# A two-layer hybrid encoder on one core: another beginning, and fused attention logits with VectorE doing the minimum and the division

## The chip, the cores and the metric

One Trainium2 chip, of which one core is used. The kernel is one program, written out without loops for that core. The metric is the device time of one execution, in microseconds. The engines are named as in the profile: PE is TensorE (matrix products), PEld its weight loads, DVE is VectorE, ACT is ScalarE, POOL is GpSimd, SP is SyncE. A small q behind a name (SPq) is the engine's sequencer, which issues DMAs and waits.

## The reference

Two layers of the same block run over two groups of tokens that share the weights: a prompt of 512 tokens and a sample of 32 tokens that continues a cache of 256. The model width is 1024, everything is float32. One layer is, with P = rmsnorm(x) @ w_in split by columns:

```
A: u = glu_a * sigmoid(glu_b); causal depthwise convolution (31 taps); layernorm; swish; @ w_conv_out
B: rotary(q), rotary(k), retention in chunks with decay (8 heads of 64); groupnorm; * silu(gate); @ w_ret_out
C: rmsnorm per head of q and k; forgetting attention, 8 heads of 64:
     s = q.k/8 + cum(logf)_query - cum(logf)_key, masked causally; softmax(s) @ v; @ w_fox_out
x = x + (sig(gA)*A + sig(gB)*B + sig(gC)*C) @ w_out
x = x + (gelu(causal dwconv3(h W_a)) * (h W_b)) @ W_down,  h = rmsnorm(x)
```

The outputs are both groups' x and the new states (convolution tails, retention states, keys, values, log forget gates).

## The kernel before, in words

Activations lie transposed: 128 channels on the partitions, the 544 tokens (32 + 512) along the free side, so 1024 channels are eight tiles of 128 x 544. Every float32 product is made of three fast ones: a matrix is split into a high part (rounded to the fast format) and a low part (what is left), and `gemm` (line 310 issues its products) adds high x high, high x low and low x high into one PSUM tile `acc`, in two halves of 272 columns. A product of the trace is thus 128 x 128 weights by 272 columns; a weight "unit" of eight 128 x 128 blocks is 48 of them. There are 2 of these PSUM tiles, so the unit after next waits until a result has been copied out.

The weights come as a stream of units (`Stream`, lines 182 to 240). `load` brings a unit from memory into `raw` (SyncE's queue, 2 buffers); `split_part` makes `hi` by a copy on ScalarE (line 203). For the low part there are two ways: usually ScalarE writes `lo = -hi` (line 206) and a DMA issued by GpSimd adds the weights from memory to it (line 207); with `sub` given, VectorE subtracts (line 209). `ahead` splits one unit and loads three units in front of the one in use.

The beginning (lines 405 to 428) loads the input tiles `xk`, the layer's parameters `par` and the first units, splits each input tile with its gain (`norm.split`, ScalarE line 328 and VectorE line 329), and squares the tiles for the norm: two on ScalarE (line 379), six on GpSimd (line 377), added up by VectorE (line 381). `norm.finish` multiplies the sum of squares with a matrix of ones (line 391) and takes the root; the result `R` scales what the products yield, so products can start before it is known. The first two units' results are therefore copied out of PSUM unscaled by ScalarE (line 449). Unit 2 and those behind it take the usual way with the GpSimd DMA.

After a unit's products `slot` hands the result to a function that evicts it. Side work (the depthwise convolution, line 488, the attention, the retention) is written as generators that `tick` advances a step at a time between pieces of the products, and `after(fn, n)` runs a function n units later. The program's text gives the priority; a planner that simulates the engines may move an instruction ahead on its engine's queue where its operands are ready early.

The attention (`fox_side`) works through 32 tiles of the prompt in each layer, one per head and query block of 128; the tile of query block qb has n = 128 (qb + 1) keys, so 128, 256, 384 or 512 columns. `p_scores` makes the products of queries and keys (line 747); VectorE writes the negated logit, key bias minus query bias minus product (line 753), adds a mask of 1e30 on the last 128 columns (line 754) and takes the minimum along the row (line 680). ScalarE makes exp(minimum - logit) with its sum (line 682), VectorE takes 1/sum (line 684), ScalarE multiplies by it (line 685). `p_trans` transposes the tile on TensorE (line 761; one PSUM tile, emptied by ScalarE at line 763), `p_pv` multiplies with the values (line 779). Three steps lie between a tile's logits and its transposes. The key biases are rows read back from memory and spread over the partitions (`ck`). Beside it run the convolution of 31 taps (VectorE line 488, partly ScalarE 491 and GpSimd 495) and the rotary turns, whose halves are swapped by DMAs (line 808) and multiplied and added on GpSimd (lines 811 and 813).

## Time and profile before

| | |
|---|---|
| median of 3 runs | 1995.84 us (1991.99 to 1999.47) |
| the profiled execution | 1999.15 us, its span 1997.0 us |
| mean granted TensorE clock | 0.991 of full speed |
| busy: PE / PEld | 1951.2 / 1909.6 us |
| busy: ACT / DVE / POOL | 1062.5 / 950.5 / 425.3 us |

How to read it: the span is the time from the first to the last instruction of one profiled execution. Busy times are shares of it, but matrix products are pipelined and their ends are modelled, so TensorE's pace is better read from how many products fall into a stretch. A row of a group of instructions gives the line, the engine, the operation, output<-input, the shapes, the count, then the busy time in us and the mean duration of one in ns, and behind the last bar the time in us that the engine was idle before them and what ended it. The chain of waits goes back from the last instruction, at each step to what released it; "issue" in it is time in which the engine waited for nothing that the profile shows.

### The profile page before, as it was taken

To read this page: it belongs to the slowest core of one execution; us is meant where nothing else is said; L and a number is where in the kernel's file an instruction comes from. 1 tells how busy PE (TensorE), PEld (TensorE's weight loads), DVE (VectorE), ACT (ScalarE), POOL (GpSimd) and SP (SyncE) were. 2 spreads that over 40 slices of the span, in tenths; PEclk is the share of its full clock that TensorE was granted. 3 is DMA by queue.
4 is the path that set the end of the run, shared out by engine and by line. 5 is a ranking of instruction groups with operands and counts; after the bars stand their busy time and mean duration, and the time that the engine had idled before them with its cause. 6 is when DMAs were issued, how large, how long until landed. Compare 5 with 4: busy or idle time off the path is not lost.

```text
span 1997.0 us, 37750 instructions
## 1 busy us (share of the span) xinstructions
PE 1951.2 (98%) x15832; PEld 1909.6 (96%) x15832; DVE 950.5 (48%) x1641; ACT 1062.5 (53%) x1462; POOL 425.3 (21%) x580
## 2 busy tenths in 40 slices
PE   7999999999999999999999998999999999999999
PEld 6999889999999999999999987999999999999999
DVE  4377978555234330233224869784543343303330
ACT  5475664476455543454555666636654554434442
POOL 2142422121111221122112334121211122112211
PEclk8999999999999999999999999999999999999999
DMA  7786646567787787787987775556778877777786
GB/s 226 173 186 163 155 106 135 133 153 164 177 218 175 173 179 174 174 176 176 209 205 160 191 172 127 127 122 146 152 169 197 197 175 174 178 173 177 174 184 141
DMA packets 105717, 337.91 MB, mean 169 GB/s; under 512 B 17628, under 2 KB 19276, under 8 KB 105164
## 3 DMA queue, kind: packets, MB, share of 16 engines
q0 software_dynamic: 41760, 152.06, 45.6%
q1 hardware_dynamic: 63788, 183.44, 27.8%
q8 instruction: 124, 2.03, 0.4%
q14 instruction: 45, 0.37, 0.1%
HBM read 321.11 MB, written 9.89 MB: 166 GB/s over the span
## 4 chain that ended last, share of the span: by engine, by line
PE 80%; issue 6%; DVE 6%; ACT 2%; DMA 2%; POOL 2%; SPq 1%; DVEq 0%; POOLq 0%; ACTq 0%
PE acc L310 75%; DVE w L488 3%; DMA lo<-in_wpack_dram 1%; PE s L747 1%; DMA w<-q 1%; PE o L779 1%; DVE w L754 1%; PE t L761 1%; DVE w L753 1%; POOL lo L207 1%; DMA w<-cscr 0%; DVE mn L680 0%; POOL w L377 0%; ACT lo L206 0%; PE s L866 0%
## 5 line engine op out<-in xcount | busy, mean ns | idle before, releaser
L310 PE MATMUL acc<-q,hi 128*128 128x272 f32 x9344 | 1791.3, 291 | 12.7 <-ACT q L328 7.6
L310 PEld LDWEIGHTS acc<-q,hi 128*128 128x128 f32 x9344 | 1478.4, 190 | 27.1 <-ACT q L328 8.7
L310 PE MATMUL acc<-q,lo 128*128 128x272 f32 x4672 | 1352.2, 290 | 5.7 <-DMA lo<-in_wpack_dram 5.4
L310 PEld LDWEIGHTS acc<-q,lo 128*128 128x128 f32 x4672 | 884.4, 190 | 6.8 <-DMA lo<-in_wpack_dram 6.3
L203 ACT ACTIVATE hi<-raw 128x1024 fp32r<-128x1024 f32 (+1 forms) x293 | 309.8, 1057 | 655.5 <-PE acc L310 654.0
L207 POOL DMA_DIRECT2D lo<-in_wpack_dram x290 | 251.7, 868 | 1264.6 <-ACT lo L206 1174.9
L206 ACT ACTIVATE lo<-hi 128x1024 fp32r<-128x1024 f32 x290 | 305.1, 1052 | 4.4
L488 DVE SCALAR_TENSOR_TENSOR w<-w,par 128x574 f32<-128x574 f32 x208 | 198.4, 954 | 3.8
L1177 DVE TENSOR_TENSOR q<-acc,q 128x544 f32<-128x544 f32 x32 | 23.2, 725 | 218.6 <-PE acc L310 218.6
L399 DVE TENSOR_TENSOR w<-acc,R 128x544 f32<-128x544 f32 x94 | 67.7, 720 | 120.2 <-PE acc L310 118.4
L1136 DVE TENSOR_TENSOR w<-acc,R 128x32 f32<-128x32 f32 x44 | 8.5, 192 | 154.6 <-PE acc L310 154.1
L1144 DVE SCALAR_TENSOR_TENSOR w<-w,par 128x546 f32<-128x546 f32 x44 | 34.7, 788 | 83.5 <-ACT w L1143 83.5
L1146 ACT ACTIVATE w<-w 128x546 f32<-128x546 f32 x44 | 29.1, 662 | 70.5 <-DVE w L1145 70.5
L682 ACT ACTIVATE w<-w,mn 128x128 f32<-128x128 f32 (+4 forms) x68 | 37.7, 555 | 31.4 <-DVE mn L680 29.0
L326 DVE TENSOR_TENSOR q<-w,q 128x544 fp32r<-128x544 f32 x44 | 31.9, 725 | 33.7 <-ACT q L325 33.7
L335 DVE TENSOR_TENSOR wr<-w,wr 128x544 fp32r<-128x544 f32 x24 | 26.5, 1104 | 42.7 <-ACT wr L334 42.7
L495 POOL TENSOR_TENSOR w<-w 128x574 f32<-128x574 f32 x24 | 40.1, 1670 | 19.8 <-ACT w L491 19.2
L357 DVE SCALAR_TENSOR_TENSOR w<-s,w 128x272 f32<-128x272 f32 (+1 forms) x60 | 23.6, 435 | 43.4 <-ACT w L354 42.9
L1016 DVE SCALAR_TENSOR_TENSOR w<-w,acc 128x544 f32<-128x544 f32 x32 | 23.0, 720 | 43.6 <-PE acc L310 43.3
L685 ACT ACTIVATE w<-w,rs 128x128 f32<-128x128 f32 (+4 forms) x68 | 37.4, 554 | 9.6 <-DVE rs L684 9.2
L753 DVE SCALAR_TENSOR_TENSOR w<-ck,CM,s 128x128 f32<-128x128 f32 (+3 forms) x64 | 34.3, 536 | 13.4 <-PE s L747 13.4
L811 POOL TENSOR_TENSOR w<-w,cst 128x544 f32<-128x544 f32 x16 | 27.1, 1693 | 56.4 <-DMA w<-q 56.4
(203 smaller groups left out, 1434.7 us busy)
## 6 DMA issues: line engine op xcount, KB each, us to landing
raw<-in_wpack_dram SPq DMA_DIRECT2D x291, 512.0 KB, 3.4
lo<-in_wpack_dram POOLq DMA_DIRECT2D x290, 512.0 KB, 5.5
w<-in_x_dram SPq DMA_DIRECT2D x16, 272.0 KB, 5.2
out_dram<-w SPq DMA_DIRECT2D x16, 272.0 KB, 4.7
w<-q SPq DMA_DIRECT2D x64, 68.0 KB, 4.0
ck<-cscr SPq DMA_DIRECT2D x16, 256.0 KB, 4.2
xn<-q SPq DMA_DIRECT2D x8, 272.0 KB, 5.3
w<-xn SPq DMA_DIRECT2D x8, 272.0 KB, 5.8
```

Of the source, the lines that this page charges most:

```text
L203: act(hi[:, sl], self.raw[u][:, sl], AF.Copy)
L206: act(lo[:, sl], hi[:, sl].bitcast(F32), AF.Copy, scale=-1.0)
L207: nc.gpsimd.dma_start(lo[:, sl], wpack[u][:, sl], accum_op=ALU.add)
L310: mm(acc[:, h, :HN], w, half(x, h), start=(i == 0 and j == 0), stop=(i == n - 1 and j == len(passes) - 1))
L326: vtt(lo, src, hi.bitcast(F32), op=ALU.subtract)
L399: vtt(two(out), acc, two(self.R), op=ALU.mult)
L488: stt(c, u[:, k : k + CO], pcol(w + k), c, op0=ALU.mult, op1=ALU.add)
L495: gtt(p, p, t, op=ALU.add)
L682: act(L[:, :n], L[:, :n], AF.Exp, scale=-1.0, bias=mn, accum_out=sm)
L685: act(L[:, :n], L[:, :n], AF.Copy, scale=rs)
L753: stt(L[:, :n], c[:, :n], CM[:, h, qb : qb + 1], p[:, :n], op0=ALU.subtract, op1=ALU.subtract)
L1144: stt(c, a[:, 1 : 1 + FO], pcol(w + 1), c, op0=ALU.mult, op1=ALU.add)
```

## The change

In the beginning, 14 products of ones with ones are issued into a PSUM tile that nobody reads. The order of loads, splits and squares is fixed as it is written (`manual_schedule`). The parameters and unit 0's weights are loaded by ScalarE's queue; the inputs and units 1 to 3 by SyncE's, unit 2 into a tile of another pool. Units 1 and 2 are split with VectorE's subtraction. All eight squares are ScalarE's. The constants, one load before, become three, pinned in SyncE's queue behind units 4 to 6. In the attention, the factor of the queries is negated and the query's bias left out (a constant along a row falls out of the softmax). VectorE's `tensor_tensor_reduce` adds product and key bias and takes the minimum at once: over the first n - 128 columns with the bias, over the last 128 with bias plus mask, which GpSimd adds beforehand (`ck_diag`). The multiply by 1/sum is VectorE's. The values' transposes in the attention use the PSUM bank `o` in place of `s`; the tag `vs` has one buffer in place of two. A zero fill on GpSimd, the load of the cache and a product with the retention state are pinned to their place in the program.

```diff
-            dma(self.raw[u][:, sl], wpack[u][:, sl])
+            (eng or dma)(self.raw[u][:, sl], wpack[u][:, sl])
...
-    act(warm, epst, AF.Copy)
-    dma(xk[0], x_in[:, 0, :])
-    ws.load_part(0, 0)
-    dma(par, params[0])
...
-    after(lambda: (tc.keep_in_program_order(dma(cst, consts)), act(blkr, blk, AF.Copy)), 3)
...
-    ws.split_part(1, 0, vtt, 1)
-    for k in range(8):
-        norm.square(k, xk[k], k not in (0, 1))
+    adma = nc.scalar.dma_start
+
+    junk = psT_t()
+    for _ in range(14):
+        mm(junk[:, 0:P], ones, ones, start=True, stop=True)
+    with tc.manual_schedule():
+        adma(par, params[0])
+        for k in range(3):
+            dma(xk[k], x_in[:, k, :])
+        ws.load_part(0, 0, eng=adma)
+        ws.load_part(0, 1, eng=adma)
+        act(warm, epst, AF.Copy)
+        for k in range(3, 8):
+            dma(xk[k], x_in[:, k, :])
+        ws.load(3)
+        norm.split(0, xk[0])
+        ws.split_part(0, 0, vtt)
+        norm.split(1, xk[1])
+        norm.split(2, xk[2])
+        ws.split_part(0, 1, vtt)
+        for k in range(3, 8):
+            norm.split(k, xk[k])
+        for u in (1, 2):
+            ws.split_part(u, 0, vtt, 1)
+        for k in range(8):
+            norm.square(k, xk[k])
+
+    def load_consts(a, b):
+        after(lambda: tc.keep_in_program_order(dma(cst[:, a:b], consts[:, a:b])), 4)
+
+    after(lambda: load_consts(C_DQ, C_ALL), 1)
+    after(lambda: load_consts(C_M2, C_DQ), 2)
+    after(lambda: load_consts(0, C_M2), 3)
...
-        nc.gpsimd.memset(fwr.bitcast(F32), 0.0)
+        tc.keep_in_program_order(nc.gpsimd.memset(fwr.bitcast(F32), 0.0))
...
-                    t = psS_t()
+                    t = bank()
...
-        nc.vector.tensor_scalar(gq8, pcol(P_GQ), 0.125, None, op0=ALU.mult)
+        nc.vector.tensor_scalar(gq8, pcol(P_GQ), -0.125, None, op0=ALU.mult)
...
+            def ck_diag(h, qb):
+
+                if h < 8 and (h, qb) not in ckm:
+                    t = wpool.tile([P, P], F32, tag="cm", name="cm", bufs=4)
+                    gtt(t, ck(h)[:, qb * P : (qb + 1) * P], cmask, op=ALU.add)
+                    ckm[h, qb] = t
+                return ckm.get((h, qb))
...
-                act(L[:, :n], L[:, :n], AF.Copy, scale=rs)
+                nc.vector.tensor_scalar(L[:, :n], L[:, :n], rs, None, op0=ALU.mult)
...
-                stt(L[:, :n], c[:, :n], CM[:, h, qb : qb + 1], p[:, :n], op0=ALU.subtract, op1=ALU.subtract)
-                vtt(L[:, n - P : n], L[:, n - P : n], cmask, op=ALU.add)
-                softmax(L, n)
+
+                m = ck_diag(h, qb)
+                if qb < 3:
+                    ck_diag(h, qb + 1)
+                mn = [spool.tile([P, 1], F32, tag="mn" + x, name="mn", bufs=4) for x in "ab"]
+                at = BIG
+                for x, o, e, t in ((c[:, : n - P], 0, n - P, mn[0]), (m, n - P, n, mn[1])):
+                    if e > o:
+                        nc.vector.tensor_tensor_reduce(L[:, o:e], x, p[:, o:e], 1.0, at, ALU.add, ALU.min, t)
+                        at = t
+                softmax(L, n, mn[1])
+                if qb == 1 and h % 2 and h < 7:
+                    ck(h + 1)
+                if qb == 3 and h % 2 == 0 and h < 6:
+                    ck(h + 3)
+                if qb == 3 and h % 2 and h < 7:
+                    ck_diag(h + 1, 0)
+                    ck_diag(h + 2, 0)
```

## Rows read from the trace of the kernel before

**Rows 1.** The page, part 1: busy us, share of the span and instructions of each engine.

```profile
PE 1951.2 (98%) x15832; PEld 1909.6 (96%) x15832; DVE 950.5 (48%) x1641; ACT 1062.5 (53%) x1462; POOL 425.3 (21%) x580
```

**Rows 2.** The chain of waits in order of time: start us, us, what. One run of weight products in the feed-forward part.

```profile
617.22 396.86 PE acc L310 x3168
```

**Rows 3.** Busy time of each engine by stretches (instructions in brackets), then the granted TensorE clock, the DMA share and GB/s.

```profile
130.00:170.00 40.00, 36.49 (x288) 35.62 (x287) 37.14 (x43) 22.20 (x34) 14.12 (x15) 0.96 0.83 211
170.00:265.00 95.00, 88.15 (x725) 78.11 (x724) 75.47 (x158) 59.72 (x133) 38.09 (x28) 0.96 0.59 138
...
490.00:1020.00 530.00, 530.00 (x4227) 529.69 (x4226) 169.75 (x295) 261.59 (x301) 94.96 (x177) 1.00 0.82 186
```

**Rows 4.** Groups of instructions from 0 to 45 us: the weight products, by which half of the weights they use.

```profile
L310 PE MATMUL acc<-q,hi 128*128 128x272 f32 x110 | 26.1, 350 | 9.5 <-ACT q L328 6.2 <-DVE q L329 3.4
...
L310 PE MATMUL acc<-q,lo 128*128 128x272 f32 x54 | 16.1, 343 | 5.4 <-DMA lo<-in_wpack_dram 5.4
```

**Rows 5.** The chain of waits in order of time, cut at 45 us.

```profile
24.20 8.90 DMA lo<-in_wpack_dram
33.14 2.63 PE acc L310 x10
35.78 1.81 PE s L391 x4
37.59 7.49 PE acc L310 x55
```

**Rows 6.** TensorE's instructions in order of time, up to 45 us: start us, us, what, and in square brackets the idle time before and what ended it.

```profile
12.54 0.39 PE L310 MATMUL acc<-q,hi 128*128 128x272 f32 x1 [1.09 <-DVE q L329]
...
15.60 0.59 PE L310 MATMUL acc<-q,hi 128*128 128x272 f32 x1 [2.05 <-DVE q L329]
...
20.98 4.52 PE L310 MATMUL acc<-q,hi 128*128 128x272 f32 x32
...
33.14 0.59 PE L310 MATMUL acc<-q,lo 128*128 128x272 f32 x1 [5.39 <-DMA lo<-in_wpack_dram]
```

**Rows 7.** Stretches of 10 us, columns as in rows 3.

```profile
10.00:20.00 10.00, 6.86 (x32) 6.32 (x31) 9.90 (x10) 3.67 (x6) 7.20 (x6) 0.75 0.67 238
...
30.00:40.00 10.00, 6.86 (x30) 6.39 (x31) 0.90 (x3) 3.81 (x6) 1.16 (x2) 0.66 1.03 333
```

**Rows 8.** The parameters' load in SyncE's queue, and ScalarE's first split that waits for it (in order of time, from two answers).

```profile
1.65 0.43 SPq L411 DMA_DIRECT2D par<-in_params_dram  x1
...
5.38 0.75 ACT L328 ACTIVATE q<-w,par 128x544 fp32r<-128x544 f32 x1 [0.36 <-DMA par<-in_params_dram]
```

**Rows 9.** Groups of instructions: the first four from 0 to 45 us (VectorE's and ScalarE's half of an input split, a half unit's and a unit's high part), the others from the whole trace.

```profile
L329 DVE SCALAR_TENSOR_TENSOR q<-w,par,q 128x544 fp32r<-128x544 f32 x8 | 9.2, 1177 | 0.2 <-ACT q L328 0.2
L328 ACT ACTIVATE q<-w,par 128x544 fp32r<-128x544 f32 x8 | 5.6, 741 | 0.8 <-DMA par<-in_params_dram 0.4 <-DMA w<-in_x_dram 0.2
L203 ACT ACTIVATE hi<-raw 128x512 fp32r<-128x512 f32 x2 | 1.3, 630 | 0.2
L203 ACT ACTIVATE hi<-raw 128x1024 fp32r<-128x1024 f32 x5 | 5.3, 1057 | 4.2 <-PE acc L310 3.4 <-DMA raw<-in_wpack_dram 0.8
...
L329 DVE SCALAR_TENSOR_TENSOR q<-q,par 128x544 fp32r<-128x544 f32 x24 | 18.8, 785 | 21.9 <-ACT q L328 21.9
...
L379 ACT ACTIVATE w<-q 128x544 f32<-128x544 f32 x21 | 13.5, 643 | 0.0
```

**Rows 10.** The GpSimd DMAs of line 207 over the whole trace, 290 of them.

```profile
DMA to landing us min/median/max: 5.0/5.5/9.1
```

**Rows 11.** The attention's operations over the whole trace. First three lines of code with least, median and longest duration in ns; then groups (mean ns behind the busy time); the last is a multiply by scalars in the convolution.

```profile
L753 DVE SCALAR_TENSOR_TENSOR w<-ck,CM,s x64: 319/534/750, 175.3 to 1268.8; 128x128 f32<-128x128 f32 x16, 128x256 f32<-128x256 f32 x16, 128x384 f32<-128x384 f32 x16, 128x512 f32<-128x512 f32 x16
L754 DVE TENSOR_TENSOR w<-w,cst x64: 266/284/1495, 175.7 to 1270.0; 128x128 f32<-128x128 f32 x64
L680 DVE TENSOR_REDUCE mn<-w x68: 257/453/687, 171.7 to 1270.9; 128x1 f32<-128x128 f32 x16, 128x1 f32<-128x256 f32 x16, 128x1 f32<-128x384 f32 x16, 128x1 f32<-128x512 f32 x16
...
L754 DVE TENSOR_TENSOR w<-w,cst 128x128 f32<-128x128 f32 x64 | 29.2, 456 | 0.8
L753 DVE SCALAR_TENSOR_TENSOR w<-ck,CM,s 128x256 f32<-128x256 f32 x16 | 7.5, 472 | 4.1 <-PE s L747 4.1
L753 DVE SCALAR_TENSOR_TENSOR w<-ck,CM,s 128x128 f32<-128x128 f32 x16 | 5.4, 337 | 2.2 <-PE s L747 2.2
L685 ACT ACTIVATE w<-w,rs 128x128 f32<-128x128 f32 (+4 forms) x68 | 37.4, 554 | 9.6 <-DVE rs L684 9.2
L486 DVE TENSOR_SCALAR w<-w,par 128x574 f32<-128x574 f32 x8 | 4.6, 570 | 0.0
```

**Rows 12.** The chain of waits by line, share of the stretch: first 130 to 300 us, then 1110 to 1270 us.

```profile
by line: PE acc L310 30.2%; DVE w L488 10.7%; issue 10.0%; DMA w<-q 5.7%; DVE w L754 4.5%; DVE w L753 3.6%; PE o L779 3.5%; DVE mn L680 3.5%; PE t L761 3.4%; PE s L747 3.0%; DMA w<-cscr 3.0%; SPq L808 2.2%; DVE q L812 2.0%; SPq L662 1.5%; A
...
by line: PE acc L310 32.8%; issue 10.5%; DVE w L488 10.1%; PE s L747 5.4%; PE t L761 3.5%; DVE w L754 3.3%; PE o L779 3.1%; DMA w<-cscr 2.7%; DVE w L753 2.6%; DMA w<-q 2.3%; DVE mn L680 2.2%; SPq L662 2.1%; DVE q L812 1.7%; SPq L808 1.5%; P
```

**Rows 13.** Groups: GpSimd's rotary multiplies over the whole trace, and VectorE's 1/sum from 170 to 265 us, one per tile.

```profile
L811 POOL TENSOR_TENSOR w<-w,cst 128x544 f32<-128x544 f32 x16 | 27.1, 1693 | 56.4 <-DMA w<-q 56.4
...
L684 DVE RECIPROCAL rs<-sm 128x1 f32<-128x1 f32 x26 | 4.1, 158 | 6.8 <-ACT w L682 6.7
```

**Rows 14.** What TensorE waited for over the whole trace: us in total, times, longest us.

```profile
PE t L761 <- ACT w L763: 5.1, 4, 1.9
PE s L625 <- DVE w L357: 4.2, 2, 2.1
```

More of the change, by code (lines that the diff above doesn't have):

```diff
@@ L407, in trunk @@
     warm = cpool.tile([P, 1], F32, name="warm")
-    act(warm, epst, AF.Copy)
-    dma(xk[0], x_in[:, 0, :])
-    ws.load_part(0, 0)
-    dma(par, params[0])
-    for k in (1, 2):
-        dma(xk[k], x_in[:, k, :])
-    ws.load_part(0, 1)
-    for k in range(3, 8):
-        dma(xk[k], x_in[:, k, :])
-    ws.load(1)
-    after(lambda: (tc.keep_in_program_order(dma(cst, consts)), act(blkr, blk, AF.Copy)), 3)
-    norm.split(0, xk[0])
-    ws.split_part(0, 0, vtt)
-    norm.split(1, xk[1])
-    norm.split(2, xk[2])
-    ws.split_part(0, 1, vtt)
-    for k in range(3, 8):
-        norm.split(k, xk[k])
-    ws.split_part(1, 0, vtt, 1)
-    for k in range(8):
-        norm.square(k, xk[k], k not in (0, 1))
+    adma = nc.scalar.dma_start
[28 more added lines that the diff above has]
+    after(lambda: load_consts(0, C_M2), 3)
+    after(lambda: act(blkr, blk, AF.Copy), 6)
     for l in range(DEPTH):
@@ L613, in qk_done, with v_done @@
             return done
-        def v_done(vt, vs, j, out):
+        def v_done(vt, vs, j, out, bank):
             def done(acc):
@@ L648, in trunk @@
         extra_n[0] = 1
-        fvs = spool.tile([P, 512], F32, tag="vs", name="vs")
+        fvs = spool.tile([P, 512], F32, tag="vs", name="vs", bufs=1)
         for j in range(4):
-            slot(rhs, v_done(fv, fvs, j, o_fv[l]))
+            slot(rhs, v_done(fv, fvs, j, o_fv[l], psO_t))
         foh, fol = qhl
```

25 lines of the change are left out of this document (15 added, 10 removed).

## The prediction

> **What bounds the kernel now.** I read the page's totals first, then the engines' busy time by stretches, then the chain of work that ended last. TensorE is busy for 98% of the span [rows 1], but its ends are modelled, so I count products instead. In the long feed-forward run 3168 weight products follow each other in 396.86 us, 0.1253 us each [rows 2]; from 490 to 1020 us no engine but TensorE matters, at full clock [rows 3]. Time can be gained where that pace is missed: in the beginning, and from 130 to about 300 us (and once more in the second layer), where VectorE is 93% and 79% busy [rows 3].
>
> The beginning: up to 45 us the trace has 110 + 54 = 164 weight products [rows 4], worth 164 x 0.1253 = 20.5 us, and four passes over a matrix of ones, 1.81 us at half clock [rows 5], so about 0.9. The chain ends that part at 37.59 + 7.49 = 45.08 us [rows 5]. So 45.1 - 21.4 = 23.7 us are lost there, in three ways. First, the input splits: TensorE idles 6.2 us at first [rows 4] and 2.05 us before 15.60 [rows 6]. Second, the clock: from 10 to 20 us it was granted 0.75 of full speed, from 30 to 40 us 0.66 [rows 7], that is, at the lower of its two levels (1.2 and 2.4 GHz) for part of the time; the ten products from 33.14 took 2.63 us [rows 5] and not 1.25. It fell after the idle 2.05 us and after 5.39 us, and after 15.60 it was back for the run that begins at 20.98, while after the idle 1.09 us before 12.54 the products were quick [rows 6]. Third, the low half of the third weight unit, which a GpSimd DMA adds up: issued at 24.20, landed 8.90 us later [rows 5], and TensorE waited 5.39 us for it [rows 6].
>
> **The change, part by part.** *The beginning.* (a) Parameters and the first weights go to ScalarE's queue, so parameters are issued first and not third. Before, they were issued at 1.65 and awaited until 5.38 [rows 8]; 3.7 us from a first issue at about 0.75 gives 4.5, 0.9 us earlier. The first activation split follows it. (b) The squares leave GpSimd. With GpSimd adding beside it the VectorE half of a split took 1.177 us; elsewhere the same operation takes 0.785 [rows 9]. Eight of these and two half-unit splits (0.74 each, the same scaled from 544 to 512 columns) are 7.8 us. VectorE starts when ScalarE's first split is done, 4.5 + 0.74 [rows 9] = 5.2, and ends at 13.0. The six products of the last block, 0.75, end unit 0 at 13.8. (c) 14 products of ones on ones run from about 1.0 us. They keep TensorE from idling before this. One pass of 128 columns costs at half clock 128/272 of a ones pass (1.81/4 = 0.45 [rows 5]), 0.21; 28 passes are 6.0 us, so they end by 7.0, when VectorE has split one block and has 6 us of splits ahead: they cost nothing, and if the cover were gone they would cost about a microsecond, from the first weights at 5.9 (4.5 + 0.74 + 0.63) on. (d) Units 1 and 2 are split by VectorE and no longer wait for a GpSimd DMA. ScalarE: eight splits 0.741, two half units 0.63, then two units at 1.06 [rows 9], 4.5 + 5.9 + 1.3 + 2.1 = 13.8, and 0.8 of waiting for their loads as before [rows 9], 14.6; then eight squares of 0.64 [rows 9], to 19.7, and the copy of unit 0's result out of PSUM, about as long, to 20.4, on which unit 2 waits for a bank. Unit 1 runs 13.8 to 19.8, unit 2 from 20.4 to 27.3 with the ones in it. What is late next is unit 3: its split (2.1 us of ScalarE) ends at 22.5, and its DMA takes 5.0, 5.5 or 9.1 us (least, median, most [rows 10]), landing at 27.5 to 31.6. At the median TensorE idles 0.7 us and the 20 products left of the 164 end at 28.0 + 2.5 = 30.5; at the worst it idles 4.3 us, the clock falls, and as long a slow run as from 15.60 to 20.98 costs 2.7 more: they end near 37. Gain 14.5, at worst 8. I take 13, by the median of 290 such DMAs and with something for the order on ScalarE, which is the planner's. The constants (1.6 MB in one load before) come in three parts behind units 4 to 6, one unit's raw load more per unit; I cost that at nothing, hidden by the two-unit lead, 0 to 3 us if it isn't.
>
> *The attention.* Each of 64 prompt tiles loses, on VectorE, the logit (median 0.534), the mask add (mean 0.456) and the minimum (0.453) [rows 11]: 1.44 us. It gets a fused logit-and-minimum over the last 128 columns, and one over the rest in 48 of 64. The trace has no fused operation. Lower bound: as the plain logit of the same width, 0.337, and 0.472 x 0.75 for the others, 256 columns on average [rows 11], together 0.69; upper: as a logit and a separate minimum, 0.69 + 0.45 = 1.14, and a wait of the second part on the first, 0.1 or so. I take 0.85, nearest the logit, since both read the same operands. It also gets the multiply by 1/sum, whose ScalarE form goes (0.554 x 68 = 37.7 us of ScalarE over both layers [rows 11]). On VectorE the nearest row is a two-scalar multiply of 574 columns at 0.570, so 0.32 for the mean tile of 320 columns if all scales, 0.57 at most, 0.2 at least. So VectorE's sum per tile goes from 1.44 to 0.85 + 0.32 = 1.17 (0.9 to 1.8): 64 x 0.27 = 17 us less (23 more to 35 less). In the chain of waits the lines of logit, mask and minimum hold 11.6% of 170 us in the first layer and 8.1% of 160 us in the second [rows 12], 33 us; the share of this that goes is (1.44 - 0.85)/1.44 = 41%, 13.5, and the multiply, which now stands in VectorE's queue, gives some back. TensorE's own needs take over in part. I take 9 of it: range 6 lost to 25 gained.
>
> The mask adds go to GpSimd, 64 of 128 columns; scaled from its 544-column add, 1.693 [rows 13], 0.4 each, 13 us a layer beside 38 of 95 us busy [rows 3]: off the path. But the trace shows that they collide: the mask add on VectorE has a median of 0.284 and a maximum of 1.495, while the logit, which reads PSUM, never exceeds 0.750 [rows 11]. The Trainium skill (SBUF — State Buffer, "SBUF: two separate sides") says why: VectorE and GpSimd take a shared port pair as an exclusive lock for a whole instruction, if VectorE has two SBUF inputs or runs in a 2-port mode. The trace agrees for two inputs; whether the multiply counts as 2-port no row shows, and by the rule it could wait as the mask add did.
>
> *Other places.* The value transposes use another PSUM bank: they waited 4.2 us on VectorE in all [rows 14]; the pins on early memsets, loads and a state product move work to where it is traced and may hold the small forget-gate product 1 us per layer. I take 2 gained together (2 lost to 6 gained).
>
> **Sum.** 13 + 9 + 2 = 24. The profiled execution took 1999.15 us (span 1997.0), 3.3 above the median of 1995.84. So 1975 for an execution like it, and 1972 in the median's frame, which I forecast.
>
> **Rivals.** *R1, only the beginning pays.* The multiply and the collisions eat what the fused operation saves: at the mask add's own stretch, 0.456 - 0.266 = 0.19 x 64 = 12 us of VectorE, more than the 9. For it: VectorE is at 79% there whatever is fused. Against: the 7.7 us a layer that mask adds hold in the first layer's chain. Time 1996 - 13 = 1983. *R2, slower: GpSimd's order.* A mask add stands in GpSimd's queue behind the rotary multiplies, which wait for their swap loads, 56.4 us in all [rows 13]; VectorE's fused operation would wait, and the convolution behind it. The masks are traced one query block ahead, two tiles, and 26 tiles took 95 us [rows 13], so 7.3 us; it decides when a load wait (56.4/16 = 3.5 on average) and two such adds (3.4) exceed that, and 6.9 is close. If half of 56.4 falls on VectorE: 1996 - 13 + 28 = 2011. *R3, TensorE runs free in the attention.* With 18 us of ScalarE less per layer also the copies of transposed tiles come sooner (5.1 us of waits [rows 14]), and the fused form costs only its lower bound: 25 and not 9, so 1956. *R4, the gain is taken back:* unit 3 is late by 4.3 us and the clock with it, the constants add 3, and the attention gains nothing: 1996 - 8 + 3 = 1991.
>
> **How the numbers follow.** Forecast 0.55, R1 0.18, R2 0.06, R3 0.14, R4 0.07. The forecast's own range is 1963 to 1982; with R1 and R3 it reaches from 1954 to 1989, leaving out R2 and part of R4 and R3. A run tells 0.5%, 10 us, from no change: all of the forecast and R3 and two thirds of R1 are faster, 0.81; the rest of R1 and R4 no change, 0.12; R2 with small mishaps slower, 0.07.
>
> **What would show it.** In the profile after: unit 0's last product near 13.7 us and the 164th near 31; a full clock from 10 to 27 us; unit 3's first product the only long wait on a low half. Splits on VectorE at 0.79, not 1.18. In 170 to 265 us (14 us earlier) more products per stretch, fused operations of 0.34 to 0.6 with no stretch, a multiply of 0.2 to 0.57. Wrong would be a wait of the fused operation on GpSimd (R2), a third wait for a low half, or a VectorE still at 79% and more with the same count of products (R1).

## The result: 0.55% slower, and the profile after

The changed kernel took 2005.47 us (median of 6 runs, 2003.59 to 2010.22), the kernel before 1994.53 in its runs beside it: ratio 1.0055, interval 1.0037 to 1.0072. 1972 was forecast, with 1989 as the upper end. So it is slower, if by little. One execution of an experiment below, the one with independent parts and no pin, took 7252.86 us and is left out of its time.

To see where the time went I set the starts of the n-th weight product in both traces side by side; the number of products is the same (14016). This table is worked out from the products' times in the trace. Each number is the run's lead over the kernel before at that point (minus: ahead), after so many weight units. Units 17 to 36 and 162 to 184 are the two attention stretches.

| after unit | 5 | 9 | 17 | 36 | 149 | 162 | 184 | 291 |
|---|---|---|---|---|---|---|---|---|
| changed kernel | -13.7 | -9.4 | -9.4 | -0.4 | -0.7 | +3.6 | +11.1 | +9.3 |

So the beginning gave 13.7; 4.3 were lost in each layer's forget gate (before units 9 and 162), the attention lost 9.0 and 7.5, and 2.1 came back elsewhere: 9.3 in all.

**The beginning.** TensorE's timeline with the waits between its instructions, then VectorE's rows of the splits:

```profile
1.06 6.17 PE L415 MATMUL t<-ones 128*128 128x128 f32 x28 [1.06 <-DVE epst L178]
7.72 0.39 PE L313 MATMUL acc<-q,lo 128*128 128x272 f32 x1 [0.21 <-DVE lo L212]
10.45 0.39 PE L313 MATMUL acc<-q,hi 128*128 128x272 f32 x1 [0.22 <-DVE q L332]
29.00 0.39 PE L313 MATMUL acc<-q,lo 128*128 128x272 f32 x1 [1.32 <-DMA lo<-in_wpack_dram]
...
9.61 3.56 DVE L332 SCALAR_TENSOR_TENSOR q<-w,par,q 128x544 fp32r<-128x544 f32 x5
```

Of the long waits of [rows 6] one is left, of 1.32 us, on the low half of unit 3, the first that a GpSimd DMA makes. A split takes 3.56/5 = 0.71 us against 1.177 [rows 9]. The stretches (busy us of each engine, then granted clock, DMA share, GB/s) answer to [rows 7]:

```profile
10.00:20.00 10.00, 9.78 (x78) 9.56 (x78) 9.19 (x13) 9.24 (x16) 0.00 (x0) 1.00 0.68 242
20.00:30.00 10.00, 8.68 (x65) 8.20 (x64) 4.50 (x9) 8.85 (x12) 1.88 (x2) 1.00 0.84 202
30.00:40.00 10.00, 10.00 (x82) 10.00 (x81) 1.21 (x2) 5.74 (x7) 1.86 (x3) 1.00 0.69 179
```

The clock stays at its higher level from 10 to 40 us.

**The forget gate.** Its memset was made to wait for its place in the program. Before, it ran at 14.91 us. In the timeline of GpSimd, ScalarE, VectorE and TensorE it is now the first of a row of steps that ends with the product:

```profile
56.02 1.29 POOL L527 MEMSET q<- 128x1024 f32 x1
...
58.99 1.06 ACT L206 ACTIVATE hi<-raw 128x1024 fp32r<-128x1024 f32 x1 [3.86 <-DMA w<-in_s_conv_dram]
60.08 1.06 ACT L209 ACTIVATE lo<-hi 128x1024 fp32r<-128x1024 f32 x1
61.05 0.24 ACT L528 ACTIVATE q<-fw 128x64 fp32r<-128x64 f32 x1
...
61.32 0.23 DVE L529 TENSOR_TENSOR q<-fw,q 128x64 fp32r<-128x64 f32 x1 [0.58 <-ACT q L528]
...
61.69 5.71 PE L313 MATMUL acc<-q 128*128 128x272 f32 x32 [2.61 <-DVE q L529]
```

The memset ends at 57.31 us. ScalarE is idle then, but in its queue the copy that needs the memset (line 528) stands behind a unit's two splits, and these come at 58.99, in the rhythm of the units. So TensorE waits 2.61 us and does its 32 products in 5.71, at a granted clock of 0.71, not in 32 x 0.1253 = 4.0: 2.61 + 1.70 = 4.3.

**The attention.** To be set beside [rows 11]: lines with the least, median and longest duration in ns (the convolution before and after, the fused operation's first part, the multiply),

```profile
L488 DVE SCALAR_TENSOR_TENSOR w<-w,par x208: 791/817/3625, 135.4 to 1345.8; 128x574 f32<-128x574 f32 x104
...
L504 DVE SCALAR_TENSOR_TENSOR w<-w,par x208: 796/817/3671, 126.0 to 1355.6; 128x574 f32<-128x574 f32 x104
...
L788 DVE CUSTOM_DVE_ANT_0 w<-ck,s x48: 271/406/554, 174.0 to 1278.9; 128x128 f32<-128x128 f32 x16, 128x256 f32<-128x256 f32 x16, 128x384 f32<-128x384 f32 x16
...
L712 DVE TENSOR_SCALAR w<-w,rs x68: 274/419/1652, 165.2 to 1283.3; 128x128 f32<-128x128 f32 x16, 128x256 f32<-128x256 f32 x16, 128x384 f32<-128x384 f32 x16, 128x512 f32<-128x512 f32 x16
```

and groups of the changed kernel's operations by form, with busy us and mean ns:

```profile
L788 DVE CUSTOM_DVE_ANT_0 w<-cm,s,mn 128x128 f32<-128x128 f32 x48 | 16.3, 340 | 2.6
L788 DVE DVE_READ_ACCUMULATOR2_ANT mn<- 128x1 f32 x112 | 8.9, 80 | 0.0
L788 DVE CUSTOM_DVE_ANT_0 w<-ck,s 128x384 f32<-128x384 f32 x16 | 8.7, 543 | 4.2 <-PE s L774 4.2
L788 DVE CUSTOM_DVE_ANT_0 w<-ck,s 128x256 f32<-128x256 f32 x16 | 6.5, 407 | 1.7 <-PE s L774 1.7
L788 DVE CUSTOM_DVE_ANT_0 w<-ck,s 128x128 f32<-128x128 f32 x16 | 4.5, 279 | 3.2 <-PE s L774 3.2
L788 DVE CUSTOM_DVE_ANT_0 w<-cm,s 128x128 f32<-128x128 f32 x16 | 4.5, 279 | 2.1 <-PE s L774 2.1
```

The fused operation is as cheap as hoped: (16.3 + 8.9 + 8.7 + 6.5 + 4.5 + 4.5)/64 = 0.77 us a tile with its accumulator reads, never stretched beyond 0.554. The multiply is not: its groups hold 11.0 + 10.2 + 7.9 + 7.6 us for the four widths, 36.7/64 = 0.57 a tile, stretched up to 1.652. Yet TensorE waits more there than before. Two places show it. The first is at the attention's threshold (GpSimd's timeline, then TensorE's):

```profile
131.87 1.45 POOL L698 TENSOR_TENSOR cm<-ck,cst 128x128 f32<-128x128 f32 x2 [3.81 <-DMA ck<-cscr]
...
135.17 1.42 POOL L698 TENSOR_TENSOR cm<-ck,cst 128x128 f32<-128x128 f32 x2
136.54 0.87 POOL L210 DMA_DIRECT2D lo<-in_wpack_dram  x1
...
144.52 0.59 PE L313 MATMUL acc<-q,lo 128*128 128x272 f32 x1 [3.26 <-DMA lo<-in_wpack_dram]
```

Four mask adds, waiting for a load of the key bias, stand in GpSimd's queue ahead of the DMAs of weight halves; one lands late, TensorE idles 3.26 us, and with the slow products behind it (0.87 granted from 130 to 156 us) that unit is 6.1 late. The second place is the worst stall (VectorE, GpSimd, TensorE):

```profile
215.43 0.34 DVE L788 CUSTOM_DVE_ANT_0 w<-cm,s,mn 128x128 f32<-128x128 f32 x1
...
216.33 2.90 DVE L504 SCALAR_TENSOR_TENSOR w<-w,par 128x574 f32<-128x574 f32 x2
...
219.27 1.85 DVE L504 SCALAR_TENSOR_TENSOR w<-w,par 128x574 f32<-128x574 f32 x1
221.04 0.60 DVE L712 TENSOR_SCALAR w<-w,rs 128x384 f32<-128x384 f32 x1
221.57 0.41 DVE L788 CUSTOM_DVE_ANT_0 w<-ck,s 128x256 f32<-128x256 f32 x1
...
221.91 3.67 DVE L504 SCALAR_TENSOR_TENSOR w<-w,par 128x574 f32<-128x574 f32 x1
225.50 0.33 DVE L788 CUSTOM_DVE_ANT_0 w<-cm,s,mn 128x128 f32<-128x128 f32 x1
...
216.68 3.83 POOL L511 TENSOR_TENSOR w<-w 128x574 f32<-128x574 f32 x2
220.46 0.97 POOL L698 TENSOR_TENSOR cm<-ck,cst 128x128 f32<-128x128 f32 x1
221.98 1.69 POOL L511 TENSOR_TENSOR w<-w 128x574 f32<-128x574 f32 x1
223.34 1.62 POOL L853 TENSOR_TENSOR w<-w,cst 128x544 f32<-128x544 f32 x1
...
225.90 1.65 PE L774 MATMUL s<-q 64*128 64x512 f32 x3 [5.79 <-DVE mn L788]
```

A pair of heads has its scores in two PSUM banks. The last read of the first head's bank is at 215.43; of the second's, the first part comes at 221.57 and the last at 225.50. Three convolution operations stand before the one and a fourth before the other, 0.82 us each at the median, here 8.4 in all beside GpSimd's operations. So long an operation is not new: before, the longest took 3.625. The next scores need that bank; TensorE idles 5.79 us, and its clock falls:

```profile
220.00:223.00 3.00, 0.11 (x1) 0.00 (x0) 3.00 (x5) 0.00 (x0) 3.00 (x4) 1.00 0.11 7
223.00:233.00 10.00, 7.10 (x34) 5.94 (x34) 7.81 (x19) 3.21 (x7) 3.47 (x5) 0.66 0.48 104
```

The two attention stretches whole (units 17 to 36 and 162 to 184, the same columns), first the kernel before, then the changed one:

```profile
135.44:313.22 177.78, 167.41 (x1370) 153.18 (x1369) 145.68 (x258) 107.16 (x215) 59.66 (x48) 0.97 0.64 154
1114.74:1312.98 198.24, 188.30 (x1597) 173.41 (x1595) 159.69 (x279) 122.00 (x236) 64.26 (x53) 0.98 0.63 152
```

```profile
126.02:312.80 186.78, 172.13 (x1371) 156.52 (x1369) 143.38 (x308) 91.83 (x181) 77.47 (x80) 0.95 0.63 147
1118.38:1324.03 205.65, 194.18 (x1596) 177.51 (x1594) 157.55 (x328) 106.45 (x202) 82.48 (x85) 0.96 0.63 147
```

TensorE's idle time is the length less its busy time: 10.37 and 9.94 us before, 14.65 and 11.47 after. So 5.8 of the 16.4 us by which the two stretches grew are idle time. The other 10.6 lie in its busy time for the same products, at a lower granted clock (0.95 and 0.96 against 0.97 and 0.98); in the second layer they are the larger part by far.

### The profile page after: what moved, and what is told of

The parts are those of the page before. It is cut to its first block, busy times and chain, and to the rows that moved or that the text cites. A ratio compares the mean times of both kernels' runs of the same rounds, so it can differ in the third digit from the quotient of the medians.

```text
span 2006.1 us, 37978 instructions
## 1 busy us (share of the span) xinstructions
PE 1962.4 (98%) x15860; PEld 1917.6 (96%) x15860; DVE 938.6 (47%) x1742; ACT 1033.1 (51%) x1399; POOL 450.4 (22%) x637
## 3 DMA queue, kind: packets, MB, share of 16 engines
q8 instruction: 125, 2.05, 0.4%
## 4 chain that ended last, share of the span: by engine, by line
PE 77%; DVE 8%; issue 7%; DMA 4%; ACT 3%; POOL 1%; SPq 1%; DVEq 0%; ACTq 0%; POOLq 0%
PE acc L313 73%; DVE w L504 3%; DMA w<-q 2%; DMA lo<-in_wpack_dram 1%; PE o L821 1%; PE s L774 1%; DVE w L788 1%; PE t L803 1%; ACT lo L209 1%; DVE w L712 1%; ACT hi L206 1%; SPq L850 1%; POOL lo L210 1%; DVE w L402 0%; DVE q L402 0%
## 5 line engine op out<-in xcount | busy, mean ns | idle before, releaser
L698 POOL TENSOR_TENSOR cm<-ck,cst 128x128 f32<-128x128 f32 x64 | 40.0, 635 | 54.1 <-DVE mn L788 31.2
L805 ACT ACTIVATE w<-t 128x128 f32<-128x128 f32 (+3 forms) x64 | 27.4, 429 | 36.8 <-PE t L803 31.6
L774 PE MATMUL s<-q 64*128 64x256 f32 (+2 forms) x192 | 33.0, 379 | 11.4 <-DVE mn L788 11.4
```

The lines of the kernel that those rows point to most:

```text
L698: gtt(t, ck(h)[:, qb * P : (qb + 1) * P], cmask, op=ALU.add)
L774: mm(ps[e][:, :nn], qhl[a][own, h // 2, NS + qb * P : NS + n], khl[b][own, h // 2, NS : NS + nn], start=(i == 0), stop=(i == 2))
```

## The experiments

All were timed against the kernel before in alternation (its median 1994.95 to 1996.21). The diffs are against the changed kernel unless they say otherwise. Many edits let the planner find another order, so two runs that differ by some 3 us in the attention show nothing by that. Executions of one kernel also differ by some us, in part with the granted clock (last section), and a trace is one of them; so its leads can be some us off those of the medians.

**The new beginning alone**, put into the kernel before, with the three loads of constants.

> The kernel before with the new beginning and the three loads of constants alone. Theory (the losses lie in other parts): the 13.7 us won by the 192nd weight product stay to the end, 1994.5 - 13.7 = 1981 us. Rival (the shifted beginning makes the planner order the attention worse by itself): the lead is gone by 300 us, 1990 us or more.

1986.5 us, ratio 0.9954 [0.9938, 0.9970]. Its lead is 13.6 up to unit 17, as forecast, and 14.4 at unit 149; then layer 1's attention, of which not a line is changed, loses 5.3. TensorE is idle there for 10.6 us, hardly more than the 9.9 before, but the granted clock is 0.96 and not 0.98; from 1151 to 1165 us it is 0.63, behind an idle 1.50 us. This trace is the longest execution of six; the medians differ by 9.7. The beginning's term holds where it is made; part is gone by the end.

**Memset not kept in program order.**

```diff
-        tc.keep_in_program_order(nc.gpsimd.memset(fwr.bitcast(F32), 0.0))
+        nc.gpsimd.memset(fwr.bitcast(F32), 0.0)
```

> The changed kernel with the zero fill of the forget-gate weights no longer pinned. Theory (the pin makes ScalarE's copy of these weights queue behind the next unit's split, 4.3 us per layer): no wait before the 32 forget-gate products, 2005.5 - 8.6 = 1997 us. Rival (ScalarE would be late anyhow, since the order there is the planner's): the 2.6 us wait stays, 2005 us.

1999.61, ratio 1.0027 [1.0010, 1.0044]: 5.9 less than the changed kernel. Its lead of 14.0 lasts through the forget gate, and layer 1's forget gate loses nothing either. That pin is shown to cost 4.3 a layer (in some traces that keep it 2.8 or 2.9 in the second layer).

**Old attention operations** (logit, mask, minimum, multiply) in the changed kernel.

> The changed kernel with the attention's logits, mask, minimum and multiply as before; beginning, pins and the other bank stay. Theory (the attention's new form costs 8 to 10 us per layer between units 22 and 30): 2005.5 - 18 = 1987 us, and no 5.8 us wait for scores. Rival (the loss there comes from the pins or the other PSUM bank): 2000 us or more.

1989.73, ratio 0.9969 [0.9956, 0.9983]: the new attention costs 15.7.

**Multiply back on ScalarE**, the first theory being the collisions of VectorE and GpSimd (R1).

```diff
-                nc.vector.tensor_scalar(L[:, :n], L[:, :n], rs, None, op0=ALU.mult)
+                act(L[:, :n], L[:, :n], AF.Copy, scale=rs)
```

> The changed kernel with the multiply by 1/sum back on ScalarE. Theory of the shared port pair (the multiply and GpSimd's adds hold each other up: it took 0.57 us on average, least 0.27): most of the attention's 18 us come back, 1990 to 1995 us. Rival (what counts is that the fused operation waits for GpSimd's mask adds behind the rotary multiplies): little changes, 2001 to 2006 us.

2003.27, ratio 1.0044 [1.0023, 1.0065], 2 us less, which the intervals do not tell apart: the theory falls. The multiply is stretched, but moving it away does not bring back the 16.

**Mask adds on VectorE; old attention and no pin; mask adds on VectorE and multiply on ScalarE; no run-ahead.**

```diff
-                    gtt(t, ck(h)[:, qb * P : (qb + 1) * P], cmask, op=ALU.add)
+                    vtt(t, ck(h)[:, qb * P : (qb + 1) * P], cmask, op=ALU.add)
```

The old attention is the code of the kernel before, the multiply's edit is the one above, and without the run-ahead these lines go:

```diff
-                if qb < 3:
-                    ck_diag(h, qb + 1)
...
-                if qb == 1 and h % 2 and h < 7:
-                    ck(h + 1)
...
```

(and two more loads of `ck` and two mask adds of the same kind).

> The changed kernel with the 64 mask adds moved from GpSimd to VectorE; fused operation and multiply stay. Theory (GpSimd's queue: mask adds stand between the rotary multiplies, wait there for loads of ck and for a free cm tile, and VectorE, TensorE and SyncE's swap loads wait behind them): the two attention stretches, which cost 7 and 10 us, cost at most 4 in all, 1992 to 1996. Rival A (the fused operation itself, in two chained parts with an accumulator read, is what VectorE has no room for): the adds put 64 x 0.28 = 18 us more on VectorE, 2008 to 2018. Rival B (the run-ahead loads of ck and their place in SyncE's queue): no change, 2003 to 2007. In the waits, the rows of the mask add's tile waiting for the fused operation and for ck's load go from GpSimd under the theory.

> The changed kernel with the old attention logits, mask, minimum and multiply, and the forget gate's memset not kept in program order: new beginning, other bank for the value transposes, kept cache load and state product. Theory (terms add): 13 from the beginning and about 6 from the bank, attention near 0, so 1978 to 1983, below every kernel so far. Rival (what the bank gives is taken back in the attention whatever feeds it, as in the run with the new beginning alone): 1986 to 1990.

> The changed kernel with the mask adds on VectorE and the multiply by 1/sum back on ScalarE: of the new attention only the fused logit and minimum and the order of the ck loads are left. Theory (GpSimd's queue, with 2 us for the multiply as the run with the multiply on ScalarE alone gave): 1988 to 1994. Rival A (the fused operation): 2003 or more. Rival B (order of the ck loads): 2001 to 2005.

> The changed kernel without the run-ahead: each mask add is traced where its tile's fused operation is, and ck loads where first needed, as before the change. Theory (GpSimd's queue): each fused operation now waits for an add that is issued later in GpSimd's order, so the attention costs more, 2008 to 2025, and VectorE's fused operation shows waits on GpSimd. Rival B (the run-ahead loads and adds hold SyncE's and GpSimd's queues): 1990 to 1998.

Mask adds on VectorE: 1996.11 [0.9994, 1.0014]; old attention and no pin: 1984.06 [0.9923, 0.9962]; mask adds on VectorE and multiply on ScalarE: 2003.15 [1.0022, 1.0054]; no run-ahead: 2009.04 [1.0045, 1.0088]. The old attention with the new beginning beats both kernels, a little above its range. With the mask adds on VectorE the wait for the weight half that came at 144 us is down to 0.5, and the time is 9.4 us less: their place in GpSimd's queue has a price, though VectorE's order differs too (three convolution operations at the second place, not four). But the stall of TensorE on a score bank is still there (5.5 us in that run's waits), and with the multiply moved as well the gain is gone; so GpSimd's queue is not the whole. The run-ahead is no culprit: without it the time is no better. It lies in the range that the theory of GpSimd's queue gave, but the sign of that theory, a wait of VectorE's fused operation on GpSimd, is not in the trace.

**Independent fused parts**, because a convolution operation often stands between a tile's two parts (in the changed kernel's trace something stands there in 24 of 48 tiles, in 14 of them a convolution operation).

```diff
-                at = BIG
...
-                        nc.vector.tensor_tensor_reduce(L[:, o:e], x, p[:, o:e], 1.0, at, ALU.add, ALU.min, t)
-                        at = t
+                        nc.vector.tensor_tensor_reduce(L[:, o:e], x, p[:, o:e], 1.0, BIG, ALU.add, ALU.min, t)
+                if n > P:
+                    vtt(mn[1], mn[0], mn[1], op=ALU.min)
```

> The changed kernel, but the second fused operation of a tile no longer takes the first one's minimum: both start from a constant, and a 128x1 minimum joins them (48 small VectorE operations more). In the changed kernel's order other VectorE work stands between the two parts of 24 of 48 tiles, 14 times a convolution operation; here no convolution operation does. Theory (the chain: a tile's PSUM bank is read to the end only by the second part, which waits for the first, and VectorE fills that gap with a convolution operation of 0.8 to 3.7 us, so TensorE gets its score bank late, idles and loses its clock): the waits of the scores for the fused operation fall under 5 us in all from 11.4, and the time to 1990 to 1998. Rival A (the fused operation and its accumulator read in themselves, whatever stands between): 2003 to 2008, the waits as before. Rival B (VectorE has no room for more operations): 2008 or more.

> The same with the forget gate's memset not kept in program order. The run without that order alone took 6 us off the changed kernel; if the two add, this takes 5 to 6 off the run with independent parts: 1984 to 1992 under the theory of the chain, 1997 to 2002 under its rivals.

> The kernel before with the new attention alone (fused operation in chained parts, mask adds on GpSimd, multiply on VectorE, its run-ahead; the value transposes' extra tile has one buffer less, to fit). Theory (the new attention costs 7 to 10 us a layer by itself): 2008 to 2014. Rival (it costs only beside the new beginning, the bank and the kept loads): 1994 to 2000.

Independent parts: 2013.12 [1.0074, 1.0104]; the same without the pin: 2004.19 [1.0029, 1.0068]; the new attention alone in the kernel before: 2007.79 [1.0052, 1.0091]. The theory of the chain falls: no convolution operation stands between the parts any more, TensorE still idles 5.17 us at the same pair, and the time is 7.7 us longer, with 48 joining minima more on VectorE. The last run shows that the new attention is dear by itself: 12.8 us slower than the kernel before.

What these traces share is what stands on VectorE from the first tile's last fused operation to the second tile's in that pair: four convolution operations in the changed kernel, four with the mask on VectorE and the multiply on ScalarE, four with independent parts, one in the kernel before. So the next runs change the order alone, or what stretches the operations in it.

**Both tiles of a pair given their fused operations together; convolution kept in program order; the convolution's adds on VectorE; the pair without the memset's pin.**

(shortened)

```diff
-                p = it["p"]
-                L = Wt(512)
-                it["L"] = L
...
+                for e in range(2) if h % 2 == 0 else ():
+                    he, ite = h + e, (it, it["mate"])[e]
+                    L = Wt(512)
...
-                softmax(L, n, mn[1])
+                L = it["L"]
+                softmax(L, n, it["mn"])
```

For the convolution in program order, and for its adds on VectorE:

```diff
-                        stt(c, u[:, k : k + CO], pcol(w + k), c, op0=ALU.mult, op1=ALU.add)
+                        tc.keep_in_program_order(stt(c, u[:, k : k + CO], pcol(w + k), c, op0=ALU.mult, op1=ALU.add))
```

```diff
-                            gtt(p, p, t, op=ALU.add)
+                            vtt(p, p, t, op=ALU.add)
```

> The changed kernel with both tiles of a pair of heads given their fused operations together, right behind the pair's scores, and the rest of the second tile's softmax where it was: the same operations in another order. In the changed kernel's order on VectorE up to four convolution operations stand between the first and the second tile's fused operations (four at the pair in which TensorE idled 5.8 us, one there in the kernel before); here none does. Theory (order: the second tile's score bank is read only behind convolution operations, which GpSimd stretches, so TensorE idles and loses its clock): the idle 5 to 6 us near 220 us goes, and the time is 1992 to 1999. Rival (VectorE with GpSimd beside it has no room there, whatever the order; the stall moves to the next pair or to the transposes): 2002 to 2010.

> The changed kernel with every convolution operation kept behind what is traced before it on VectorE. Then they spread over all 32 tiles of a layer (42 of them stand among the tiles, 26 in the changed kernel, all of these among the 13 tiles from the 12th on), at most three between two tiles. Theory (order: convolution operations crowded ahead of a waiting tile): 1990 to 2000. Rival A (room on VectorE: more of the convolution now falls beside the attention): 2008 or more.

> The changed kernel with the convolution's 12 adds per layer on VectorE, not on GpSimd (0.75 us each there against 1.8 on GpSimd). Theory of the collisions (the idle near 220 us comes from GpSimd's two or three adds in a row, behind which convolution operations take 3 us and more): that stall shrinks to 2 us, and the time is 1996 to 2002 although VectorE has 9 us a layer more. Rival (order alone, or room on VectorE): 2005 to 2013.

> The changed kernel with the pair's fused operations together and the forget gate's memset not kept in program order. If the two add: 5 to 6 less than the run with the pair alone, so 1986 to 1994 by the theory of order, which is the range of the kernel with the old attention (1984); 1996 to 2004 by the rival.

Pair together: 1989.40 [0.9959, 0.9985]; convolution in order: 1995.77 [0.9995, 1.0020]; its adds on VectorE: 1996.39 [0.9997, 1.0028]; pair without the pin: 1983.76 [0.9929, 0.9966]. Order alone, VectorE's and with it that of GpSimd's mask adds, is worth 16.1 us, with all operations and engines as in the changed kernel. VectorE's timeline of the same pair in the run with the pair together, then TensorE's next long wait:

```profile
208.07 0.41 DVE L787 CUSTOM_DVE_ANT_0 w<-ck,s 128x256 f32<-128x256 f32 x1
...
208.41 0.41 DVE L787 CUSTOM_DVE_ANT_0 w<-ck,s 128x256 f32<-128x256 f32 x1
...
208.75 0.34 DVE L787 CUSTOM_DVE_ANT_0 w<-cm,s,mn 128x128 f32<-128x128 f32 x1
...
209.02 0.34 DVE L787 CUSTOM_DVE_ANT_0 w<-cm,s,mn 128x128 f32<-128x128 f32 x1
...
213.18 4.27 DVE L504 SCALAR_TENSOR_TENSOR w<-w,par 128x574 f32<-128x574 f32 x2
...
219.17 0.41 DVE L712 TENSOR_SCALAR w<-w,rs 128x384 f32<-128x384 f32 x1
...
219.73 0.72 PE L804 MATMUL t<-cst,w 128*128 128x128 f32 x3 [3.02 <-DVE w L712]
```

Both banks are free at 209.3; the convolution is stretched afterwards as much as in the changed kernel (4.27 for two), and no score waits for it. But the second tile's multiply does, and its transposes: TensorE idles 3.02 us where it idled 5.79. What TensorE waited for over the whole trace (us in total, times, longest) has one line for the scores' banks. In the kernel before, the changed kernel and the run with the pair together:

```profile
PE s L747 <- DVE w L753: 5.8, 4, 3.0
...
PE s L774 <- DVE mn L788: 11.4, 6, 5.8
...
PE s L774 <- DVE mn L787: 0.4, 1, 0.4
```

The stretches of the attention in the run with the pair together:

```profile
126.09:302.67 176.58, 165.13 (x1371) 151.20 (x1369) 144.15 (x308) 91.03 (x181) 76.89 (x80) 0.97 0.65 155
1106.54:1304.99 198.45, 186.68 (x1596) 172.32 (x1594) 155.78 (x328) 105.29 (x202) 82.29 (x85) 0.98 0.66 152
```

They are 17.4 us shorter than in the changed kernel. Only 2.9 of that is idle time (11.45 and 11.77 us are left): in their place stand waits for transposes (10.2 us for ScalarE's copies in the whole trace, 6.6 in the changed kernel, and the 3.02) and for weight halves (8.5, and 6.0). The rest is the faster pace of the same products, with the granted clock back at the level of the kernel before. So what the order took away are the longest waits and the slow products that came with them, not waiting as such.

With the convolution's adds on VectorE, the same line, and the convolution's own with least, median and longest ns:

```profile
PE s L774 <- DVE mn L788: 6.6, 5, 2.0
```

```profile
L504 DVE SCALAR_TENSOR_TENSOR w<-w,par x208: 790/817/1991, 126.4 to 1344.3; 128x574 f32<-128x574 f32 x104
```

Taking adds off GpSimd shortens the longest convolution operation from 3.671 to 1.991 and the wait from 5.8 to 2.0, at the price of more work on VectorE, and gives 9.1 us. But its order differs too: two convolution operations stand in that pair, not four. Keeping the convolution in order mends layer 0 (it loses nothing there) and still loses 8.5 in layer 1; its longest wait for a score bank is 3.4, though their sum is hardly less (11.1). So the price of the order is shown; that GpSimd's adds, by stretching the operations, are the stall's second foot is likely and not shown by itself.

**What each part is worth with the order mended** (all without the memset's pin): multiply on ScalarE; the convolution's adds on VectorE; the old operations, but both plain logits of a pair together.

The edits are those above; the last has, in the pair's loop,

```diff
+                    stt(L[:, :n], ck(h + e)[:, :n], CM[:, h + e, qb : qb + 1], ps[e][:, :n], op0=ALU.subtract, op1=ALU.subtract)
```

> The pair's fused operations together and the memset not kept in order, with the multiply by 1/sum back on ScalarE. Theory (with the order mended VectorE's sum counts, and the multiply, 0.57 us a tile with GpSimd beside it, is 18 us of it a layer): 1978 to 1982. Rival (the multiply lies beside other work, as in the changed kernel, where taking it away gave 2 us): 1982 to 1986.

> The pair's fused operations together and the memset not kept in order, with the convolution's adds on VectorE. Theory (collisions with GpSimd and the order feed the same stall: one of the two mended, the other gives little): 1981 to 1987. Rival (each has its own price, 9 us for the adds as in the changed kernel): 1973 to 1978.

> New beginning, other bank, memset not kept, old attention (plain logit, mask add, minimum on VectorE, multiply on ScalarE), with both logits of a pair together behind its scores. Against the run with the pair's fused operations it has the same order and the old operations: the difference is what the fused form is worth by itself. Theory (the logit's order matters to the fused form alone, because the old order had one convolution operation at the critical pair): 1980 to 1985, as with the old order (1984), and the fused form is worth nothing to 3 us. Rival (the fused form is worth the 9 us that were forecast, once the order is the same): 1990 or more.

Multiply on ScalarE: 1992.32 [0.9978, 1.0002]; adds on VectorE: 1979.62 [0.9904, 0.9937]; old operations: 1985.16 [0.9941, 0.9971]. The fused form with the multiply on VectorE is worth 1.4 us against the old operations in the same order, less than the runs tell apart. The multiply on ScalarE, which changed the changed kernel by no more than 2 us, adds 8.6 here: neither theory. The run with the adds on VectorE is the fastest, 0.8% faster than the kernel before, and between its two theories: 4.1 less than the pair without them, and not 9; the two intervals just overlap.

The leads over the kernel before, worked out as above, for the runs that decide:

| after unit | 5 | 9 | 17 | 36 | 149 | 162 | 184 | 291 |
|---|---|---|---|---|---|---|---|---|
| beginning alone | -13.6 | -13.6 | -13.6 | -12.8 | -14.4 | -14.4 | -9.1 | -7.8 |
| memset unpinned | -14.0 | -14.0 | -14.0 | -4.8 | -6.6 | -6.6 | -0.3 | -1.9 |
| mask on VectorE | -11.5 | -7.1 | -7.1 | -3.4 | -5.2 | -2.3 | +1.8 | +1.5 |
| old attention, unpinned | -11.6 | -11.6 | -11.6 | -14.9 | -15.2 | -15.2 | -15.2 | -13.5 |
| independent parts | -13.3 | -9.1 | -9.1 | -0.6 | -0.8 | +3.6 | +12.6 | +12.3 |
| pair together | -13.9 | -9.3 | -9.4 | -10.6 | -12.5 | -8.2 | -8.0 | -9.7 |

From unit 17 to 36 the changed kernel loses 9.0, the pair gains 1.2; from 162 to 184 it loses 7.5, the pair 0.2.

## Why the prediction was wrong

**The terms.** In the trace the beginning gave 13.7 (13 were forecast), the forget gates lost 8.6 (with the other bank, 2 were to be gained), the two attention stretches lost 16.5 (9 were to be gained), and 2.1 came back elsewhere.

**The beginning: right.** 13 was taken and 13.7 measured. Unit 0 was to end at 13.8 and unit 1 begins at 14.2; the 164th product was put at 30.5 and starts at 31.2; the splits (0.71) and the clock came as described. Unit 3's first low half is the only long wait, 1.3 us in this run and about 3 in some others (their lead at unit 5 is 9.4 to 10.5): the range was 8 to 14.5.

**The pins and the other bank: mis-sized.** "May hold the small forget-gate product 1 us per layer" named the right product; it measured 4.3, since behind the wait of 2.61 the 32 products ran at a granted clock of 0.71. By the prediction's own [rows 5] and [rows 6], where a wait of 2.05 us left slow products behind, the price of a wait should have been doubled. What the other bank gives was not taken apart. The wait of [rows 14] on which it rested (2.1 us before 147.5 and its slow products, 3.9 in all) is gone in both layers of the changed kernel. That gives 3.9 and 3.8 us within the attention's stretches, whose rest thus loses 24.2 and not 16.5. But with the old bank it went in both layers in the run with the new attention alone, and in the first in the run with the new beginning alone, where the second kept 2.1 us of it.

**The attention: the step that failed.** "The share of this that goes is (1.44 - 0.85)/1.44 = 41%, 13.5 ... I take 9 of it." The fused operation's duration was not at fault: 0.85 was 0.77. The multiply's 0.32 was 0.57, its stated upper end, so VectorE's sum fell from 1.44 to 1.34 a tile and not to 1.17; by the prediction's own way (33 x 0.10/1.44) that would have left a gain of some 2. But the runs show a loss of 16, which this sum of durations does not give. The chain of waits was read as if VectorE's time there went with its operations, in an order that stays. The worst of TensorE's waits ended when a bank's last reader came in VectorE's queue, and with other operations the planner queued up to four convolution operations before it; behind the long waits came slow products. Order alone turns 2005 into 1989.

**The rivals.** R2 named the right side and a time near the result (2011), with a chance of 0.06, and a part of its mechanism is there: mask adds waiting in GpSimd's queue. But what they held up was a weight half's DMA, not the fused operation, and with the adds on VectorE the bank's stall stayed. R1's collisions exist. The Trainium skill (SBUF — State Buffer, "SBUF: two separate sides") has VectorE and GpSimd take a shared port pair as an exclusive lock when VectorE reads two operands from SBUF or runs in a 2-port mode. The traces agree for the convolution (two operands in SBUF, 0.817 at the median and 3.671 at most) and for the fused operation, which reads PSUM and never exceeded 0.554; for the multiply, which the prediction left open, 1.652 at most speaks for the lock. The multiply took 0.57 - 0.32 = 0.25 a tile more than forecast, 16 us over 64 tiles, where R1 reckoned 12 of VectorE's time; but R1 forecast no loss from it, and the loss came with the order. R3's sooner copies did not come: the transposes' waits for ScalarE are 6.6 us in all, and were 5.1. R4's late unit 3 did not come either (1.32).

**What stays open.** Why moving the multiply to ScalarE costs 7 to 9 us in two orders and not in the changed kernel's. In all three it adds 6 us to TensorE's waits for ScalarE's copies of transposed tiles (7.2 to 13.3 in the changed kernel, 11.5 to 17.4 with the mask adds on VectorE, 13.7 to 19.7 in the pair without the pin), and in the changed kernel the waits for score banks fall by nearly as much (11.4 to 6.1); that this is the whole reason is not shown. Open too: why the changed kernel's planner put the second tile so late, and why the clock falls behind some waits and not behind others of the same length.

## What to carry to other kernels

Where an in-order engine serves both a waiting producer and long filler work, look up in the order of its queue what stands ahead of each buffer's last reader: trace the readers of all banks of a group right behind their producer, and leave the filler behind them. What work saved on an engine is worth is not known until that order is known, and any edit may change it; so compare the queue's order of two versions before comparing their sums. A wait of 2 to 3 us on TensorE can cost 1.6 to 1.9 times its length (2.1 cost 3.9, 2.61 cost 4.3, 3.26 cost 6.1), where the products behind it run at the lower clock. They do not always: in the pair without the pin a wait of 2.95 us near 1120 left the granted clock at 1.00 and cost 3.2.

## What the runs showed of the hardware that was not expected

A fused add-and-minimum on VectorE costs 0.279 us for 128 columns, 0.407 for 256 and 0.543 for 384, with a read of the accumulator of 0.080 that follows at once; with its starting value taken from a tile and not a constant, the 128 columns cost 0.340. A multiply by one scalar per row, in SBUF alone, of 128 to 512 columns, varied from 0.274 to 1.652 us; that GpSimd beside it is the cause was not tried by itself. A convolution operation of 0.82 us took 3.67 while two GpSimd operations ran one behind the other; with GpSimd's adds taken away the longest took 1.99. And executions of one kernel can differ by the granted clock: the six of the new beginning alone took 1982.28 us at 0.998 to 1990.99 us at 0.993, and time multiplied by clock is 1977 to 1978 in all six. In other kernels part of the difference is left: in the ten of the pair together it is 1973 to 1979, of times from 1984.52 to 1994.56.
